# A two-block transformer kernel on one core: the opening of the first FFN by single k tiles, for four blocks, in a fixed order of vector and scalar work

## Chip, cores and metric

The kernel runs on one core of one Trainium2 chip. The metric is the device time of one execution in microseconds (us); lower is better. Before the change the median of three runs is 1663.18 us (1662.93 to 1663.85).

## What is computed

Two residual networks follow each other on one sequence x of 256 tokens and 1024 columns, in fp32. Each has two layers. What matters here is the first sublayer of the first layer: a SwiGLU FFN on a normalized and modulated x.

```python
c_act = jax.nn.silu(c)
for l in range(DEPTH):
    mod = (c_act @ w_ada[l] + b_ada[l]).reshape(B, N_SUB, 3, D_MODEL)

    def norm_mod(h, j):
        shift = mod[:, j, 0][:, None, :]
        scale = mod[:, j, 1][:, None, :]
        return _rms(h) * g_norm[l, j] * (1.0 + scale) + shift

    x = x + 0.5 * gate(0) * _swiglu(norm_mod(x, 0), w_ffn_up[l, 0], w_ffn_down[l, 0])
    x = x + gate(1) * _mixer(norm_mod(x, 1), ...)
    x = x + 0.5 * gate(2) * _swiglu(norm_mod(x, 2), w_ffn_up[l, 1], w_ffn_down[l, 1])
```

`_swiglu` is (silu(h Wg) * (h Wu)) Wd with 2816 inner columns. The second network has two layers of another mixer and another FFN, and its own modulation `w_mod_2`. Before any matmul of the first FFN can run, the kernel therefore needs x, its mean square, the row silu(c), and for each 128 columns of x the shift and the scale, which are dot products of silu(c) with rows of `w_ada`.

## The kernel before

**Precision.** TensorE multiplies fp32r, a rounded fp32. Each weight piece of 128 rows by 1024 columns (a "unit", 0.5 MB) is split into `hi` (ScalarE, a copy that rounds, L247) and `lo` = raw - hi (VectorE, L248). The activations are split in the same way into `hTh` and `hTl`, stored transposed: 8 k tiles of 128 columns of x, each 128 by 256 tokens. A product is hi*hTh + hi*hTl + lo*hTh, three matmuls.

**Weights.** `enqueue` lists loads of two units (1 MB) in the order of use, `pump` issues the load on SP's queue into one of four `raw` buffers and emits hi and lo into eight buffers each; a buffer is free again when TensorE has used its unit (`free`). 

**An FFN** works in 11 blocks of 256 inner columns. For a block, `gemm_ch` runs 4 units (2 k tiles each) with 24 matmuls of 256 columns each into two PSUM banks (gate and up), `act_ch` computes silu(gate) * up and splits it, and `down_both` runs two more units against the result. 

**Modulation.** `mod_piece` loads 1 MB of `w_ada` into a raw buffer and forms two columns of 128 dot products: on VectorE as one product with a running sum (L282), or, if `spread` says so, as a product on GpSimd (L279) and a sum on ScalarE (L280). 

**The opening** of the first FFN (`start`, `ffn_open`) handles three blocks. `start` loads silu's row c spread over 128 partitions (0.5 MB), the columns of small constants `cols`, the first w_ada piece, x and the identity, all on SP's queue, and computes the root mean square and the normalized x (`norm_in`). `ffn_open` then goes in four steps q of two k tiles: pieces for shift and scale of step q+1 (one column on VectorE, one on GpSimd and ScalarE, since `spread` is 1), hi and lo, the transposed x scaled and shifted (`norm_fill`: ScalarE L370, VectorE L375 and L376), and the matmuls of blocks 0, 1 and 2. After it, block 3 runs in the ordinary way, then the downs of blocks 0 to 2, and so on. From `hooks[3]` on, 14 pieces of w_ada for the following sublayers and some constants (`late_start`) are worked in between.

**What sets the order.** TensorE's order is the order of the program's text. The order on the other engines and queues is set by a scheduler with priorities (`high_priority`). 

```python
self.gemm_ch(ps[j], unit, q)                                     # L469
nc.gpsimd.tensor_tensor(sl, sl, self.crow, ALU.mult)             # L279
nc.scalar.activation(out=hi[:, :width], in_=r, func=ACTF.Copy)   # L247
```

Of the kernel before, what the change touches and what calls it, by code (L numbers as in the profile page):

```python
# [39 lines left out]
EXP_LN = "natural_log_exp_and_others"  # L40
GELU = "gelu_apprx_tanh_and_others"
# [32 lines left out]
LEAD = 3  # L74
MUL = 0
# [30 lines left out]
class Net:  # L106
# [54 lines left out]
    def start(self, pieces):  # L161
# [5 lines left out]
        self.ident = self.con("ident")  # L167
        self.nones = self.const.tile([P, 128], F32, name="nones")
# [7 lines left out]
        self.load_c(0)  # L176
        nc.sync.dma_start(out=self.cols, in_=self.a["cols"])
        pieces[0]()
        nc.sync.dma_start(out=self.x, in_=self.a["x"].rearrange("p (t d) -> p t d", t=2))
        nc.sync.dma_start(out=self.ident, in_=self.a["cst"][:, 0:128])  # L180
        pieces[1]()
        self.identr = self.const.tile([P, 128], F32R, name="identr")
        nc.vector.tensor_copy(self.identr, self.ident)
        with self.hot():
            return [self.norm_in(t, True) for t in range(2)]
# [7 lines left out]
    def late_start(self):  # L193
# [5 lines left out]
        nc.vector.tensor_copy(self.masks, m[:, 0:N_MASK])  # L199
        t, y, z, z2 = [self.sm(8, f"sp{i}", 1) for i in range(4)]  # L200
        lam = self.col("lam", 0, 8)
        nc.scalar.activation(out=t, in_=lam, func=ACTF.Abs)
# [16 lines left out]
        nc.vector.tensor_scalar(self.brh, self.col("b_r", 0, 16), 0.5, None, ALU.mult)  # L219
        self.gq8 = self.const.tile([P, 2], F32, name="gq8")  # L220
        nc.vector.tensor_scalar(self.gq8, self.col("g_qk", 0, 2), 0.125, None, ALU.mult)
# [9 lines left out]

    def pump(self, count=8):
# [3 lines left out]
        while self.queue and self.emitted < end:  # L236
            src, n, width = self.queue[0]
            if src is not None:
                raw = self.raw()
                nc.sync.dma_start(out=raw[:, :n * width], in_=src)  # L240
                self.cur, self.pos = raw, 0
                self.queue[0] = (None, n, width)
# [3 lines left out]
            with self.tc.high_priority(offset=0 if self.opening else -COLD):  # L246
                nc.scalar.activation(out=hi[:, :width], in_=r, func=ACTF.Copy)  # L247
                nc.vector.tensor_tensor(lo[:, :width], r, hi[:, :width].bitcast(F32), ALU.subtract)  # L248
# [6 lines left out]
    opening = True  # L255
    spread = 2
# [82 lines left out]
    def norm(self, t, ss=None, early=False):  # L339
# [5 lines left out]
        if early:  # L345
            self.nc.gpsimd.tensor_tensor(ms, ss[:, 0:1], ss[:, 1:2], ALU.add)
            self.nc.gpsimd.tensor_tensor(ms, ms, self.eps, ALU.add)
        else:
            self.nc.vector.scalar_tensor_tensor(ms, ss[:, 0:1], EPS, ss[:, 1:2], ALU.add, ALU.add)  # L349
        return self.rstd(ms, 1, "rs")  # L350

    def norm_in(self, t, scalar=False):
        r = self.norm(t, None, scalar)
        xn = []
        for n in range(2):
            h = self.s2()
            src = self.x[:, t, n * 512:(n + 1) * 512]
            if scalar and (t or MUL):
                self.nc.scalar.activation(out=h, in_=src, func=ACTF.Copy, scale=r[:, 0:1])
            else:  # L360
                self.nc.vector.tensor_scalar(h, src, r[:, 0:1], None, ALU.mult)
            xn.append(h)
# [87 lines left out]
    def ffn_open(self, xn, mod, pieces, act_ch):  # L450

        ps = [[self.up(), self.up()], [self.dn(), self.dn()], [self.dn(), self.dn()]]

        def turn(q):
            bank = self.tp()
            for t in range(2):
                for i in range(2):
                    sl = slice((q % 2 * 2 + i) * 128, (q % 2 * 2 + i + 1) * 128)
                    self.nc.tensor.transpose(bank[:, (2 * t + i) * 128:(2 * t + i + 1) * 128], xn[t][q // 2][:, sl],
# [1199 lines left out]
```

## Time and profile before

| | |
|---|---|
| median of three runs | 1663.18 us |
| the profiled execution | 1661.24 us |
| its span, first to last instruction | 1659.5 us |
| TensorE busy (PE) | 1600.4 us, 96% |
| VectorE busy (DVE) | 1273.3 us, 77% |
| ScalarE busy (ACT) | 859.7 us, 52% |
| GpSimd busy (POOL) | 69.8 us, 4% |
| granted TensorE clock, mean | 0.992 |

Engines wait for each other by semaphores. In a list of waits each row says which engine and line waited, for which instruction, for how long in all, how many times and for how long at most. In a timeline, each row has the start and the duration in us, the engine, the line of the code, the operation, the tiles written and read, the shape, a count if several instructions were merged, and in brackets how long the engine sat idle before it and which instruction ended that. Matmul durations overlap, so their pace is read from their starts.

### The profile page before, as it was taken

The numbers are of one execution on the slowest core, as the hardware profiler recorded it, in microseconds if no ns is written. First come the engines' busy times: TensorE is split into PE (matmuls) and PEld (weight loads), VectorE is DVE, ScalarE is ACT, GpSimd is POOL, SyncE is SP. The second block draws the span as 40 slices with busy tenths as digits, with TensorE's granted clock in tenths as the row PEclk, the third lists the DMA queues.
The fourth block names the chain that finished last, engine by engine and source line by source line (L and its number), as shares of the span: only waits on it lengthen the run. The fifth ranks groups of instructions, "written<-read, shape, count | busy, mean of one in ns | idle before, by whom it ended". The sixth has DMA issues, their size and how long they took to land.

```text
span 1659.5 us, 26626 instructions
## 1 busy us (share of the span) xinstructions
PE 1600.4 (96%) x10574; PEld 1448.0 (87%) x10574; DVE 1273.3 (77%) x2160; ACT 859.7 (52%) x1378; POOL 69.8 (4%) x70
## 2 busy tenths in 40 slices
PE   3899999999999999999999999999999999999998
PEld 3889987889999899989789999887899989789997
DVE  7878688679887888776689787687888776786554
ACT  4634456764344443457664445556544465564442
POOL 3100010000000000000000000001000010000000
PEclk9999999999999999999999999999999999999999
DMA  7889768449887699855349887534788854258550
GB/s 294 298 328 359 300 211 310 142 135 365 334 333 284 252 353 345 310 194 175 115 165 364 334 303 295 188 112 146 290 329 315 328 185 169 79 173 307 178 190 27
DMA packets 59325, 411.36 MB, mean 248 GB/s; under 512 B 6640, under 2 KB 7360, under 8 KB 11712
## 3 DMA queue, kind: packets, MB, share of 16 engines
q1 hardware_dynamic: 59200, 409.66, 67.0%
q8 instruction: 83, 1.36, 0.3%
q14 instruction: 42, 0.34, 0.1%
HBM read 408.54 MB, written 1.09 MB: 247 GB/s over the span
## 4 chain that ended last, share of the span: by engine, by line
PE 83%; DVE 9%; ACT 3%; issue 1%; DMA 1%; POOL 1%; SPq 0%; POOLq 0%; DVEq 0%; ACTq 0%
PE up L435 13%; PE up L436 13%; PE up L437 13%; PE dn L446 8%; PE dn L445 8%; PE dn L448 8%; DVE lo L248 3%; PE dn L421 2%; PE dn L424 2%; PE dn L422 2%; PE up L421 2%; PE up L424 2%; PE up L422 2%; DVE raw L282 1%; PE dn L437 1%
## 5 line engine op out<-in xcount | busy, mean ns | idle before, releaser
L247 ACT ACTIVATE hi<-raw 128x1024 fp32r<-128x1024 f32 (+1 forms) x508 | 527.3, 1058 | 438.3 <-PE up L436 154.2
L248 DVE TENSOR_TENSOR lo<-raw,hi 128x1024 fp32r<-128x1024 f32 (+1 forms) x508 | 618.6, 1236 | 171.0 <-ACT hi L247 167.5
L435 PE MATMUL up<-hTh,hi 128*128 128x256 f32 x1984 | 560.7, 283 | 8.4 <-DVE hTh L375 8.4
L436 PE MATMUL up<-hTl,hi 128*128 128x256 f32 x1984 | 558.0, 281 | 1.5 <-DVE hTl L376 1.5
L437 PE MATMUL up<-hTh,lo 128*128 128x256 f32 x1984 | 557.6, 281 | 0.0
L435 PEld LDWEIGHTS up<-hTh,hi 128*128 128x128 f32 x1984 | 374.3, 189 | 12.0 <-DVE hTh L375 8.8
L436 PEld LDWEIGHTS up<-hTl,hi 128*128 128x128 f32 x1984 | 374.5, 189 | 4.2 <-DVE hTl L376 2.0
L437 PEld LDWEIGHTS up<-hTh,lo 128*128 128x128 f32 x1984 | 374.6, 189 | 0.0
L282 DVE SCALAR_TENSOR_TENSOR raw<-raw,crow 128x1024 f32<-128x1024 f32 x234 | 281.3, 1228 | 3.8 <-DMA raw<-in_w_ada 3.4
L445 PE MATMUL dn<-hi,s 128*128 128x512 f32 x552 | 218.6, 396 | 0.0
L446 PE MATMUL dn<-lo,s 128*128 128x512 f32 x552 | 217.6, 394 | 0.0
L448 PE MATMUL dn<-hi,s 128*128 128x512 f32 x552 | 173.7, 394 | 0.0
L448 PEld LDWEIGHTS dn<-hi,s 128*128 128x128 f32 x552 | 103.7, 188 | 24.4
L446 PEld LDWEIGHTS dn<-lo,s 128*128 128x128 f32 x552 | 103.7, 188 | 21.5
L445 PEld LDWEIGHTS dn<-hi,s 128*128 128x128 f32 x552 | 103.7, 188 | 21.3
L533 ACT ACTIVATE s<-up 128x512 f32<-128x512 f32 (+1 forms) x60 | 32.7, 555 | 140.2 <-PE up L437 140.1
L534 DVE TENSOR_TENSOR s<-s,up 128x512 f32<-128x512 f32 (+1 forms) x60 | 37.5, 634 | 66.4 <-PE up L437 66.4
L370 ACT ACTIVATE s<-tp,shift,scale 128x128 f32<-128x128 f32 x160 | 58.6, 466 | 35.9 <-PE tp L383 26.3
L331 POOL TENSOR_TENSOR rs<-ms,mhalf 128x1 f32<-128x1 f32 x22 | 20.8, 947 | 1171.9 <-DVE ms L349 1171.7
L421 PE MATMUL dn<-hi,hTh 128*128 128x512 f32 (+2 forms) x176 | 66.2, 380 | 0.3 <-DVE hTh L375 0.3
L422 PE MATMUL dn<-lo,hTh 128*128 128x512 f32 (+2 forms) x176 | 65.2, 374 | 0.0
L424 PE MATMUL dn<-hi,hTl 128*128 128x512 f32 (+2 forms) x176 | 63.4, 375 | 0.0
(342 smaller groups left out, 1902.7 us busy)
## 6 DMA issues: line engine op xcount, KB each, us to landing
raw<-in_ffn SPq DMA_DIRECT2D x198, 1024.0 KB, 5.1
raw<-in_w_ada SPq DMA_DIRECT2D x72, 1024.0 KB, 5.2
raw<-in_mix SPq DMA_DIRECT2D x48, 1024.0 KB, 5.3
raw<-in_w_mod SPq DMA_DIRECT2D x48, 1024.0 KB, 6.8
s<-gate SPq DMA_DIRECT2D x10, 512.0 KB, 9.3
raw<-in_mix SPq DMA_DIRECT2D x4, 1032.0 KB
raw<-in_mix SPq DMA_DIRECT2D x4, 912.0 KB, 5.9
mw<-in_mix_w SPq DMA_DIRECT2D x2, 896.0 KB, 6.8
```

The lines of the kernel that those rows point to most:

```text
L247: nc.scalar.activation(out=hi[:, :width], in_=r, func=ACTF.Copy)
L248: nc.vector.tensor_tensor(lo[:, :width], r, hi[:, :width].bitcast(F32), ALU.subtract)
L282: nc.vector.scalar_tensor_tensor(sl, sl, 1.0, self.crow, ALU.mult, ALU.mult, accum_out=dst[:, b:b + 1])
L421: nc.tensor.matmul(out, xh, hi[:, sl], start=(k == 0), stop=False)
L422: nc.tensor.matmul(out, xh, lo[:, sl], start=False, stop=False)
L424: nc.tensor.matmul(out, xl, hi[:, sl], start=False, stop=(k == 7))
L435: nc.tensor.matmul(out, hi[:, sl], self.hTh[:, k], start=(k == 0 and c % 2 == 0), stop=False)
L436: nc.tensor.matmul(out, hi[:, sl], self.hTl[:, k], start=False, stop=False)
L437: nc.tensor.matmul(out, lo[:, sl], self.hTh[:, k], start=False, stop=(k == 7 and c % 2 == 1))
L445: nc.tensor.matmul(banks[t, n], xh, hi[:, sl], start=first, stop=False)
L446: nc.tensor.matmul(banks[t, n], xh, lo[:, sl], start=False, stop=False)
L448: nc.tensor.matmul(banks[t, n], xl, hi[:, n * 512:n * 512 + 512], start=False, stop=last)
```

## The change

The opening now treats four blocks (`OPEN = 4`) and one k tile at a time, eight steps instead of four.

- `start` issues loads from two engines. SP's queue gets x in two halves first, then w_ada rows and weights; ScalarE's queue gets row c as one partition (4 KB), the identity and `cols`, behind a table load for SILU.
- `open_norm` spreads row c over the partitions by two matmuls with a row of -1, takes SILU with scale -1 from PSUM, computes the mean square of x's first half on ScalarE and of the second on VectorE, and normalizes the first half on VectorE, the second on ScalarE.
- `ffn_open` loads w_ada rows for one k tile (two of 0.5 MB, in buffers of their own kind, `s4`), forms both dot products on VectorE, adds shift on ScalarE and scale on VectorE. GpSimd has no products any more. All of x is transposed at once into four banks and copied out. hTh is then written by ScalarE from the copy (in step 0 by VectorE), hTl by VectorE.
- `line` ties each vector and scalar instruction of the opening to the one before it in the program's text, so that their order there is fixed. `self.lows` holds back lo until the text asks for it.
- The weights of the first FFN are laid out for four blocks; the hooks with the 14 pieces begin at block 4. `late_start` is tied behind an activation of the FFN.

```diff
+        row = self.mw.tile([P, 1792], F32, tag="gw", name="crow0")[0:1, 0:D]
+        self.tables(SILU)
+        nc.scalar.dma_start(out=row, in_=self.a["c"][0:1, :])
+        nc.scalar.dma_start(out=self.ident, in_=self.a["cst"][:, 0:128])
+        for t in range(2):
+            nc.sync.dma_start(out=self.x[:, t], in_=self.a["x"][:, t * D:(t + 1) * D])
+        nc.scalar.dma_start(out=self.cols, in_=self.a["cols"])
...
+    def open_norm(self, row):
+
+        nc = self.nc
+        spread = [self.up(), self.up()]
+        for n in range(2):
+            nc.tensor.matmul(spread[n], self.nones[0:1, :], row[:, n * 512:(n + 1) * 512], start=True, stop=True)
+        self.crow = self.const.tile([P, D], F32, tag="crow", name="crow")
+        ss = [self.sm(1, "ss") for _ in range(2)]
+        a, v = lambda inst: self.line("a", inst), lambda inst: self.line("v", inst)
+        a(nc.scalar.activation(out=self.hTl[:, 0:4].rearrange("p k n -> p (k n)"), in_=self.x[:, 0], func=ACTF.Square,
+                               scale=1.0 / 32, accum_out=ss[0]))
+        v(nc.vector.scalar_tensor_tensor(self.hTl[:, 4:8].rearrange("p k n -> p (k n)"), self.x[:, 1], 1.0 / D,
+                                         self.x[:, 1], ALU.mult, ALU.mult, accum_out=ss[1]))
+        rs = []
+        for t in range(2):
+            ms = self.sm(1, "ms")
+            nc.gpsimd.tensor_tensor(ms, ss[t], self.eps, ALU.add)
+            rs.append(self.rstd(ms, 1, "rs"))
+        for n in range(2):
+            a(nc.scalar.activation(out=self.crow[:, n * 512:(n + 1) * 512], in_=spread[n], func=ACTF.Silu, scale=-1.0))
+        xn = [self.s4() for _ in range(2)]
+        v(nc.vector.tensor_scalar(xn[0], self.x[:, 0], rs[0][:, 0:1], None, ALU.mult))
+        for n in range(2):
+            sl = slice(n * 512, (n + 1) * 512)
+            a(nc.scalar.activation(out=xn[1][:, sl], in_=self.x[:, 1, sl], func=ACTF.Copy, scale=rs[1][:, 0:1]))
+        return xn
...
+    def line(self, engine, inst):
+
+        if self.opening:
+            self.lines = dict(self.lines)
+            if engine in self.lines:
+                self.after(inst, self.lines[engine])
+            self.lines[engine] = inst
+        return inst
...
+        def load(k):
+            landed[k] = [self.s4() for _ in range(2)]
+            for i in range(2):
+                nc.sync.dma_start(out=landed[k][i], in_=rows(i, k))
...
+        def piece(k):
+            for i, w in enumerate(landed.pop(k)):
+                if k == 0 and i == 1:
+                    v(nc.vector.tensor_scalar(plus, self.col("b_ada", 8, 8), 1.0, None, ALU.add))
+                v(nc.vector.scalar_tensor_tensor(w, w, 1.0, self.crow, ALU.mult, ALU.mult, accum_out=sums[i][:, k:k + 1]))
+            one = slice(k, k + 1)
+            a(nc.scalar.activation(out=mod["shift"][:, one], in_=sums[0][:, one], func=ACTF.Identity,
+                                   bias=self.col("b_ada", k)))
+            v(nc.vector.tensor_scalar(mod["scale"][:, one], sums[1][:, one], plus[:, one], self.col("g_norm", k), ALU.add,
+                                      ALU.mult))
+
+        load(0)
+        self.fetch(0, 2)
+        self.fetch(1)
+        load(1)
+        xn = self.open_norm(row)
...
+        def high(k, early=False):
+            g, i = k // 2, k % 2
+            src = turned[g][:, i * 256:i * 256 + 256] if early else xT[g][:, g % 2 * 512 + i * 256:g % 2 * 512 + i * 256 + 256]
+            how = dict(func=ACTF.Identity, scale=mod["scale"][:, k:k + 1], bias=mod["shift"][:, k:k + 1])
+            if early:
+                v(nc.vector.tensor_scalar(self.hTh[:, k], src, mod["scale"][:, k:k + 1], mod["shift"][:, k:k + 1], ALU.mult,
+                                          ALU.add))
+            else:
+                a(nc.scalar.activation(out=self.hTh[:, k], in_=src, **how))
+            full[k] = self.s1()
+            a(nc.scalar.activation(out=full[k], in_=src, **how))
+
+        def rest(k):
+            v(nc.vector.tensor_tensor(self.hTl[:, k], full.pop(k), self.hTh[:, k].bitcast(F32), ALU.subtract))
...
+        self.lows = []
+        piece(0)
+        self.pump(1)
+        high(0, True)
+        self.low()
...
+        for k in range(1, 8):
+            if k % 2 == 0:
+                units = self.take(OPEN)
+            if k < 7:
+                load(k + 1)
+                if k % 2:
                     self.pump(2)
-                fill(q + 1, turned[q + 1])
-            block(2, q)
-            if q < 2:
-                turned.append(turn(q + 2))
+                piece(k + 1)
+                high(k + 1)
+                if k % 2:
+                    self.low()
+                rest(k + 1)
+                if k % 2:
+                    self.low()
+                    self.pump(2)
+                    self.low(2)
+            else:
+                self.pump(4)
+                self.low(4)
+            for j in range(OPEN):
+                if k == 1 and j > 1:
+                    block(j, 0, units[j], "b")
+                block(j, k, units[j])
+                if k % 2:
+                    self.free(1)
+                if k == 7:
+                    with self.hot():
+                        act_ch(j, ps[j])
```

VectorE, the opening from the products for the second step on; `raw` or `s_` with `crow` are the products with row c, `lo` the split of weights, before first and then now:

```order
L282 SCALAR_TENSOR_TENSOR raw,shift<-raw,crow 128x1024
L376 TENSOR_TENSOR hTl<-s_168,hTh 128x2x128
L297 SCALAR_TENSOR_TENSOR shift<-shift,cols 128x2
L282 SCALAR_TENSOR_TENSOR raw,scale<-raw,crow 128x1024
L297 SCALAR_TENSOR_TENSOR scale<-scale,cols 128x2
L299 TENSOR_TENSOR scale<-scale,cols 128x2
L375 CAST hTh<-s_244 128x2x128
L376 TENSOR_TENSOR hTl<-s_244,hTh 128x2x128
L248 TENSOR_TENSOR lo<-raw,hi 128x1024 x2
```

```order
L530 SCALAR_TENSOR_TENSOR s_244,sums<-s_244,crow 128x1024
L530 SCALAR_TENSOR_TENSOR s_245,sums<-s_245,crow 128x1024
L534 TENSOR_SCALAR scale<-sums,plus,cols 128x1
L292 TENSOR_TENSOR lo<-raw,hi 128x1024
L572 TENSOR_TENSOR hTl<-s_261,hTh 128x256
L292 TENSOR_TENSOR lo<-raw,hi 128x1024 x3
L530 SCALAR_TENSOR_TENSOR s_332,sums<-s_332,crow 128x1024
L530 SCALAR_TENSOR_TENSOR s_333,sums<-s_333,crow 128x1024
L534 TENSOR_SCALAR scale<-sums,plus,cols 128x1
L572 TENSOR_TENSOR hTl<-s_341,hTh 128x256
```

Now two k tiles (steps 2 and 3) take four products, four lo, two scale steps and two hTl; in the odd step hTl follows scale with no lo between them. In the whole opening these are 16 products and 16 lo.

SP's queue, from its first load on, before first and then now:

```order
L189 DMA crow<-in_c 128x1024
L177 DMA cols<-in_cols 128x434
L274 DMA raw<-in_w_ada 128x2048
L179 DMA x<-in_x 128x2048
L180 DMA cst<-in_cst 128x128
L274 DMA raw<-in_w_ada 128x2048
L240 DMA raw<-in_ffn 128x2048
```

```order
L173 DMA x<-in_x 128x1024 x2
L518 DMA s_100<-in_w_ada 128x1024
L518 DMA s_101<-in_w_ada 128x1024
L271 DMA raw<-in_ffn 128x1024 x2
L271 DMA raw<-in_ffn 128x2048
L518 DMA s_109<-in_w_ada 128x1024
L518 DMA s_110<-in_w_ada 128x1024
L271 DMA raw<-in_ffn 128x2048 x2
L518 DMA s_244<-in_w_ada 128x1024
```

x moves from the fourth place to the first, row c and `cols` leave the queue, and the w_ada rows and the first unit go in halves of a megabyte. Up to and with `s_244`, the first row of step 2, the queue has 7.9 MB, and ScalarE's queue 0.3.

## Rows read from the trace of the kernel before

**Rows 1.** The page, busy time of TensorE, share of the span and instructions.

```profile
PE 1600.4 (96%) x10574; PEld 1448.0 (87%) x10574; DVE 1273.3 (77%) x2160; ACT 859.7 (52%) x1378; POOL 69.8 (4%) x70
```

**Rows 2.** Waits of TensorE, 0 to 100 us; total us, times, longest.

```profile
PE tp L459 <- DVE s L361: 14.4, 1, 14.4
PE up L435 <- DVE hTh L375: 8.4, 1, 8.4
...
PE tp L459 <- ACT s L359: 0.9, 1, 0.9
```

**Rows 3.** Windows, 84 to 222 us: engines busy, clock, DMA share, GB/s.

```profile
84.00:222.00 138.00, 137.77 (x924) 126.28 (x922) 104.40 (x151) 58.62 (x71) 1.07 (x1) 1.00 0.83 310
```

**Rows 4.** Timeline of TensorE, opening.

```profile
25.88 0.58 PE L435 MATMUL up<-hTh,hi 128*128 128x256 f32 x1 [8.42 <-DVE hTh L375]
...
29.44 0.41 PE L436 MATMUL up<-hTl,hi 128*128 128x256 f32 x1
29.66 0.41 PE L437 MATMUL up<-hTh,lo 128*128 128x256 f32 x1
...
34.89 0.28 PE L435 MATMUL dn<-hTh,hi 128*128 128x256 f32 x1
...
37.97 0.28 PE L437 MATMUL dn<-hTh,lo 128*128 128x256 f32 x1
...
83.51 0.39 PE L445 MATMUL dn<-hi,s 128*128 128x512 f32 x1
```

**Rows 5.** Chain of waits to 84 us: start, us, engine, what.

```profile
2.12 8.82 DMA x<-in_x
...
39.14 7.76 DMA raw<-in_w_ada
```

**Rows 6.** Timeline of VectorE, opening.

```profile
21.13 4.49 DVE L248 TENSOR_TENSOR lo<-raw,hi 128x1024 fp32r<-128x1024 f32 x2
...
28.44 0.07 DVE L282 DVE_READ_ACCUMULATOR raw<-raw,crow 128x1 f32 x1
28.62 0.16 DVE L297 SCALAR_TENSOR_TENSOR scale<-scale,cols 128x2 f32<-128x2 f32 x1
...
30.24 0.43 DVE L376 TENSOR_TENSOR hTl<-s,hTh 128x256 fp32r<-128x256 f32 x1
...
61.21 3.49 DVE L248 TENSOR_TENSOR lo<-raw,hi 128x1024 fp32r<-128x1024 f32 x3
```

**Rows 7.** Timeline of GpSimd, opening.

```profile
13.87 0.47 POOL L347 TENSOR_TENSOR ms<-ms,eps 128x1 f32<-128x1 f32 x1
14.42 0.68 POOL L331 TENSOR_TENSOR rs<-ms,mhalf 128x1 f32<-128x1 f32 x1
...
47.07 6.01 POOL L279 TENSOR_TENSOR raw<-raw,crow 128x1024 f32<-128x1024 f32 x2 [10.42 <-DMA raw<-in_w_ada]
```

**Rows 8.** Timeline of ScalarE, first instructions.

```profile
0.73 1.28 ACT L190 ACT_TABLE_LOAD   x1 [0.73 <-PEq L1648]
5.37 1.06 ACT L190 ACTIVATE crow<-crow 128x1024 f32<-128x1024 f32 x1 [3.36 <-DMA crow<-in_c]
```

**Rows 9.** Stretches before 22 us, columns as in rows 3.

```profile
2.00:4.50 2.50, 0.00 (x0) 0.00 (x0) 0.00 (x0) 0.01 (x1) 0.00 (x0) 1.00 0.70 249
4.50:22.00 17.50, 2.23 (x8) 1.43 (x8) 12.33 (x36) 10.98 (x22) 5.57 (x8) 1.00 1.01 420
```

**Rows 10.** Groups of VectorE by form: count, busy us, mean ns.

```profile
L968 DVE TENSOR_SCALAR s<-s 128x1024 f32<-128x1024 f32 x2 | 1.4, 695 | 3.0 <-ACT s L961 3.0
```

**Rows 11.** Groups of TensorE by form.

```profile
L1049 PE MATMUL dn<-s,cst 128*128 128x512 f32 x8 | 4.2, 610 | 2.6 <-DVE s L1038 2.6
```

**Rows 12.** Timeline of ScalarE, opening.

```profile
41.18 1.16 ACT L370 ACTIVATE s<-tp,shift,scale 128x128 f32<-128x128 f32 x3 [3.35 <-DVE scale L299]
```

**Rows 13.** DMA issues, 0 to 100 us: count, KB each, us to landing.

```profile
raw<-in_ffn SPq DMA_DIRECT2D x16, 1024.0 KB, 5.0
```

**Rows 14.** Stretch from 20 to 30 us, columns as in rows 3.

```profile
20.00:30.00 10.00, 3.23 (x13) 2.94 (x14) 8.92 (x13) 4.09 (x10) 4.35 (x2) 1.00 0.58 211
```

More of the change, by code (lines that the diff above doesn't have):

```diff
@@ L73 @@
 RAW = 4
-LEAD = 3
-MUL = 0
+OPEN = 4
 S4 = 8
@@ L159, in con, with start @@
         return self.cst[:, o:o + w]
-    def start(self, pieces):
+    def start(self):
         nc = self.nc
@@ L175, in start @@
         self.hTl = self.const.tile([P, 8, S], F32R, name="hTl")
[L176 to L185, printed above, removed]
+        return row
+    def open_norm(self, row):
[23 more added lines that the diff above has]
+        return xn
     def load_c(self, i):
@@ L230, in enqueue, with fetch @@
             self.queue.append((src[:, i * width:(i + n) * width], n, width))
+    fetched = None
+    def fetch(self, at, parts=1):
+        src, n, width = self.queue[at]
+        if self.fetched is None:
+            self.fetched = {}
+        if id(src) in self.fetched:
+            return self.fetched.pop(id(src))[1]
+        raw = self.raw()
+        for i in range(parts):
+            sl = slice(i * n * width // parts, (i + 1) * n * width // parts)
+            self.nc.sync.dma_start(out=raw[:, sl], in_=src[:, sl])
+        if parts > 1 or at:
+            self.fetched[id(src)] = src, raw
+        return raw
     def pump(self, count=8):
@@ L255, with low @@
     opening = True
+    lines = ()
+    def line(self, engine, inst):
+        if self.opening:
+            self.lines = dict(self.lines)
[3 more added lines that the diff above has]
+        return inst
+    def low(self, n=1):
+        for _ in range(n):
+            self.lows.pop(0)()
     spread = 2
@@ L344, in norm, with norm_in @@
         ms = self.sm(1, "ms")
[L345 to L349, printed above, removed]
+        self.nc.vector.scalar_tensor_tensor(ms, ss[:, 0:1], EPS, ss[:, 1:2], ALU.add, ALU.add)
         return self.rstd(ms, 1, "rs")
-    def norm_in(self, t, scalar=False):
-        r = self.norm(t, None, scalar)
+    def norm_in(self, t):
+        r = self.norm(t)
         xn = []
@@ L490, in ffn_open @@
         self.opening = False
-        self.spread = 2
         self.pump(4)
-        for j in range(3):
-            with self.hot():
-                act_ch(j, ps[j])
     def ffn(self, mod, hooks, nxt, opening=None):
@@ L589, in ffn @@
             nd = 1
-        start = 2 if opening is None else 3
+        start = 2 if opening is None else OPEN
         for h in sum(hooks[:start], []):
@@ L1405, in body, with first_rows @@
         self.pending = {}
-        xn = self.start([shifts[0][0], shifts[0][4]])
+        row = self.start()
+        def first_rows(i, k):
+            return a["w_ada"][0][2 * i + k // 4][:, k % 4 * 1024:k % 4 * 1024 + 1024]
         flat = list(gates[0])
```

123 lines of the change are left out of this document (73 added, 50 removed).

## The prediction

> **What bounds the kernel now.** I read the waits of TensorE first, because TensorE is busy 96% of the span [rows 1]. In the first 100 us it waits 29.5 us in six groups: 14.4 us for the normalized x, 8.4 us for hTh, three more for hi, hTl and lo, and 0.9 us for x again [rows 2]. From 84 to 222 us, the rest of the first FFN, it is busy 137.77 of 138.00 us while VectorE is busy 104.40 and the loads take 0.83 of the DMA engines [rows 3]. So what can be won in this FFN is won before 84 us, and nothing behind it waits for anything but TensorE.
>
> The timeline of TensorE gives the size of the opening. The first matmul of the FFN starts at 25.88, the first down matmul at 83.51 [rows 4]. Between them lie four blocks of 96 matmuls of 256 columns. At full clock 26 of them take 37.97 - 34.89 = 3.08 us, 0.1185 each, so 384 take 45.5 us. The missing 57.6 - 45.5 = 12.1 us are the later waits and stretches at half clock (1.2 of 2.4 GHz), for instance from 29.44 to 29.66, 0.21 us a matmul [rows 4].
>
> The chain of waits up to 84 us says what fed them late [rows 5]: x lands after 8.8 us in the queue, and further down a w_ada load of 7.8 us comes too late. The timeline of VectorE shows a second cost: a pair of lo that starts at 21.1, beside GpSimd's products with row c, takes 4.49 us, and three that start at 61.2 take 3.49, which is 1.15 from start to start [rows 6]. GpSimd has six such products, the last two from 47.1 to 53.1 [rows 7].
>
> **The change, step by step.** The opening now treats one k tile of 128 at a time, for four blocks, and every step follows from VectorE's list. So I add up that list and put TensorE behind it.
>
> *Start.* The first half of x is the first load of SP's queue. The nearest row is row c before: also half a megabyte, also first, used at 5.37 [rows 8]. So x's first half is there at 5.4, the second 0.52 MB at 420 GB/s [rows 9] later, at 6.6. VectorE squares it with its sum (1.22 us and 0.08, as lo and a read of the sum in [rows 6]): 7.9. GpSimd then adds eps (0.47) and takes the first root (0.68) [rows 7]: 9.1. One TENSOR_SCALAR of 1024 columns is 0.70 [rows 10]: the products with row c begin at 9.8.
>
> *Row c.* It comes by ScalarE's queue, is spread by two fp32 matmuls of 512 columns (0.6 us each at full clock [rows 11], twice that at half) and passes two SILU of some 0.6. ScalarE first loads a table (1.28 us from 0.73 [rows 8]). I bound its landing from two sides: some 5 us, if it doesn't stand behind SP's loads; or 10, behind 2.6 MB of them. The nearest row is the 64 KB identity, which stood behind x in one queue; here the queue is its own, so I take 5. Then the spread row is ready at some 8, under the cover of x's sums until 9.8. Landing at 10 it would be ready at 13, and 3 us would show, less the wait for loads that I add below. The Trainium skill (DMA: Bandwidth & Descriptors, Issuing engines are not separate DMA queues) says that loads started by different engines interleave on the same DMA engines and that a second engine saves issue time only. By that the bandwidth stays at 420 GB/s and the early landing of the small row holds; no row of before shows a second queue.
>
> *VectorE from 9.8 to the last hTl.* From the order of the change: 16 products with c at 1.15 from start to start, 18.4; 16 lo at 1.15, 18.4, now that GpSimd has no products; hTh once and hTl eight times at some 0.4, 3.7; eight scale steps, each 0.12 until the sum is there and 0.17, 2.4 [rows 6]. Further three waits for ScalarE: in steps 3, 5 and 7 no lo stands between scale and hTl, so VectorE waits for two ACTIVATEs of 256 columns, 0.1 + 0.36 + 0.46 + 0.06 = 1.0 each (0.35 apart in pairs of 128 columns before [rows 12]), 3.0. And one wait for loads: up to the first row of step 2 the queues move 8.2 MB, of which 0.5 are there at 5.4; 7.6 MB at 420 GB/s are 18.2, landing at 23.6, while VectorE is ready after 4 products, 4 lo and the small steps, 11.0 us, at 20.8: 2.8. Sum 18.4 + 18.4 + 3.7 + 2.4 + 3.0 + 2.8 = 48.7: the last hTl is ready at 58.5.
>
> *Loads behind that.* Until the last step they are 18.1 MB, 43 us at 420 GB/s. The order gives two steps of rows and two raw buffers ahead, so I cost later waits at nothing.
>
> *TensorE.* Its first FFN matmul starts at some 13, after two products, scale and hTh. A pair of steps is 96 matmuls, 11.4 us, against 11.6 of VectorE's list (eight at 1.15, two hTl, two scale steps, one wait), so it keeps up and ends 5.6 us (46 matmuls that come after the last hTl, and 0.1 to start) behind it: 64.1, against 83.51. **Gain 19.4 us.** The SILU table is there from the start, so the 1.28 us load that came with the first SILU of the FFN goes; it lay beside TensorE's work, nothing.
>
> *What follows.* Block 4 needs four units. Two lo precede the first SILU product on VectorE, the third and fourth follow by 65; TensorE takes 2.8 us a unit, so it doesn't wait. The 14 w_ada pieces now lie in four blocks. VectorE's 104 us in 138 [rows 3] stay; its share is the same, for all of the FFN moves forward. The late constants with two table loads (2.6 us of ScalarE, half idle) hide too. Behind the first FFN every engine's order is unchanged. So the 19.4 us reach the end: the profiled execution of 1661.24 us (span 1659.5) would take 1641.8. The median of the runs, 1663.18, lies 1.9 above it: **1643.8 us**.
>
> **Rivals.** *Half-size loads are slow.* x, the w_ada rows and the first unit now move in half megabytes. Between 2 and 4.5 us, when mostly row c (half a megabyte) moved, the rate was 249 GB/s, against 420 later [rows 9]. If all 10.5 MB of such loads move at 249 and the other 7.6 MB at 420, the last rows land at 2 + 42.2 + 18.1 = 62. Behind them come a product, scale, hTh and hTl (3.0) and the last step (5.7): 71, a gain of 12.5, 1650.7. Against it: row c was read 128 times from one place, and the queue had only just started. The Trainium skill (same page, Bandwidth) states the rule "Batch DMAs to ≥1 MiB for ≥75% of peak", which speaks against this change; by its fit of 2.0 us plus the bytes at 436 GB/s, an estimate, half a megabyte takes 3.2 us, the twenty such loads 64 us if one followed the other, and the opening would end at some 91, slower than now. The 1 MB loads of before take 5 us to land and still sum to 420 GB/s [rows 9, 13], so they overlap; I give the rival 0.13.
>
> *TensorE stays at half clock.* Before, it ran at half clock for a while after its first FFN matmul [rows 4]. Here the first two steps have waits for hi and lo between their matmuls. If their 96 matmuls all run at 0.213, they end at 13.4 + 20.4 = 33.8 and TensorE sets the pace from there: 288 x 0.1185 = 34.1, 67.9, 3.8 us later than forecast, 1647.6. Otherwise TensorE catches up before step 3, since VectorE is the slower. 0.08.
>
> *Loads wait for buffers, and it gets slower.* Row and raw buffers come free only as VectorE works through its list, and SP issues in order: a load that waits for its buffer holds up all behind it. Before, the loads moved at 211 GB/s from 20 to 30 us [rows 14]. The 18.1 MB at 211 are 86 us; the last rows land at 88 and the opening ends at 97, 13 us later than now: 1676.6. The point from which it decides: below 250 GB/s over the whole opening, the last rows land after 75 and nothing is gained. Against it: six row buffers and four raw buffers run ahead, and that stretch of before lies beside GpSimd's products, when VectorE was slow. 0.04.
>
> *The gain doesn't reach the end.* If VectorE fell behind in blocks 4 to 10, TensorE would wait there, where it had no wait. That takes 16 us of new waits in a stretch where VectorE has 34 us to spare: 1660 to 1666. 0.03.
>
> **How the numbers follow.** Forecast 0.72: an opening that ends between 59 and 68. At the low end the waits for loads and ScalarE (5.8 us) vanish; then TensorE's own 45.5 us from 13 set the end, 59, so 1639. The high end takes in half-size loads at 249 GB/s, so the range is 1639 to 1651; the half clock and a late row c lie within. Outside are the two last rivals and some of the first, less than 2 in 10. About 0.2% (3.3 us) is what a measurement can tell from no change: faster 0.93 (forecast and the first two rivals), the same 0.03, slower 0.04.
>
> **What would show it.** Right: the first FFN matmul at about 13; lo at 1.22 us everywhere; TensorE's waits in the first 100 us some 15 to 17 us, most of them before 13; the first product of step 2 waiting for a w_ada load by some 2 to 3 us; three waits of hTl for ScalarE of 1 us; block 4 from about 64; no wait of TensorE from there to the end of the first FFN, some 202 us. Wrong: products waiting for w_ada loads in step after step (first or third rival), 0.21 us a matmul after 27 us (second), or a wait of TensorE for lo or hi after 64 (last).

## The result and the profile after

The changed kernel takes 1642.05 us (median of 4 runs, 1641.78 to 1644.12), against 1663.06 us (1660.17 to 1663.85) for the kernel before beside it: a ratio of 0.9879, 95% interval 0.9862 to 0.9897. The forecast was 1643.8 us. The change itself was timed a second time later, beside other runs: 1642.82 against 1660.69 us. In the profiled execution, of 1641.78 us (span 1640.0), TensorE is busy 1601.5 us, one more than before [rows 1]: what went was idle time.

The waits of TensorE from 0 to 100 us, 29.5 us before [rows 2], are 9.3 us:

```profile
PE tp L547 <- DVE s L206: 2.7, 1, 2.7
PE up L190 <- DMA crow<-in_c: 2.6, 1, 2.6
PE up L584 <- ACT hTh L567: 1.4, 2, 1.0
PE up L584 <- ACT hi L289: 1.3, 1, 1.3
PE up L584 <- DVE hTl L572: 1.3, 3, 0.4
```

Its timeline, to set against [rows 4]: the first FFN matmul starts at 13.99 instead of 25.88, and block 4, which follows the opening, at 67.38 instead of 83.51. At 37.65 comes the last wait of the opening; soon after it, matmuls are 0.21 us apart for a while.

```profile
13.99 1.22 PE L584 MATMUL up<-hTh,hi 128*128 128x256 f32 x4 [1.29 <-ACT hi L289]
...
36.69 0.39 PE L584 MATMUL up<-hTh,hi 128*128 128x256 f32 x1 [1.03 <-ACT hTh L567]
...
37.65 0.39 PE L584 MATMUL up<-hTl,hi 128*128 128x256 f32 x1 [0.45 <-DVE hTl L572]
...
39.07 0.41 PE L584 MATMUL up<-hTh,lo 128*128 128x256 f32 x1
39.28 0.41 PE L584 MATMUL up<-hTl,hi 128*128 128x256 f32 x1
...
67.38 0.28 PE L491 MATMUL up<-hTh,hi 128*128 128x256 f32 x1
```

The timeline of VectorE, to set against [rows 6], has its list. It waits for w_ada loads three times, and in the odd steps for ScalarE before hTl. Three lo take 3.49 us as before, but no group is drawn out to 4.49 for a pair.

```profile
11.37 1.23 DVE L530 SCALAR_TENSOR_TENSOR s<-s,crow 128x1024 f32<-128x1024 f32 x1 [1.17 <-DMA s<-in_w_ada]
...
17.91 1.23 DVE L530 SCALAR_TENSOR_TENSOR s<-s,crow 128x1024 f32<-128x1024 f32 x1 [1.24 <-DMA s<-in_w_ada]
...
25.45 1.23 DVE L530 SCALAR_TENSOR_TENSOR s<-s,crow 128x1024 f32<-128x1024 f32 x1 [1.95 <-DMA s<-in_w_ada]
...
29.85 3.49 DVE L292 TENSOR_TENSOR lo<-raw,hi 128x1024 fp32r<-128x1024 f32 x3
...
37.16 0.43 DVE L572 TENSOR_TENSOR hTl<-s,hTh 128x256 fp32r<-128x256 f32 x1 [1.22 <-ACT s L569]
...
60.97 0.42 DVE L572 TENSOR_TENSOR hTl<-s,hTh 128x256 fp32r<-128x256 f32 x1 [1.22 <-ACT s L569]
```

The stretches, with the columns of [rows 3]. From 20 to 30 us the loads move 411 GB/s (211 before [rows 14]), and from block 4 to 202 us TensorE is busy all the time, as before [rows 3].

```profile
4.50:22.00 17.50, 12.70 (x61) 10.03 (x59) 11.89 (x20) 11.46 (x20) 1.71 (x4) 1.00 1.02 390
20.00:30.00 10.00, 8.95 (x69) 7.99 (x67) 7.74 (x14) 4.90 (x8) 0.00 (x0) 1.00 1.02 411
67.38:202.00 134.62, 134.62 (x915) 124.06 (x914) 109.31 (x174) 61.60 (x74) 0.00 (x0) 1.00 0.88 328
```

### The profile page after: what moved, and what is told of

It reads as the page before. It is cut to its first block, busy times and chain, and to the rows that moved or that the text cites. A ratio compares the mean times of both kernels' runs of the same rounds, so it can differ in the third digit from the quotient of the medians.

```text
span 1640.0 us, 26615 instructions
## 1 busy us (share of the span) xinstructions
PE 1601.5 (98%) x10578; PEld 1446.6 (88%) x10578; DVE 1267.4 (77%) x2163; ACT 856.3 (52%) x1372; POOL 52.5 (3%) x62
## 4 chain that ended last, share of the span: by engine, by line
PE 84%; DVE 9%; ACT 3%; DMA 2%; issue 1%; POOL 1%; SPq 0%; POOLq 0%; ACTq 0%; DVEq 0%
PE up L491 13%; PE up L492 13%; PE up L493 13%; PE dn L501 8%; PE dn L502 8%; PE dn L504 8%; DVE lo L292 2%; PE dn L477 2%; PE dn L480 2%; PE dn L478 2%; PE up L477 2%; PE up L480 2%; PE up L478 2%; PE dn L584 1%; DMA s<-in_w_ada 1%
## 5 line engine op out<-in xcount | busy, mean ns | idle before, releaser
L292 DVE TENSOR_TENSOR lo<-raw,hi 128x1024 fp32r<-128x1024 f32 (+1 forms) x508 | 609.7, 1221 | 160.9 <-ACT hi L289 157.2
L491 PE MATMUL up<-hTh,hi 128*128 128x256 f32 x1920 | 540.8, 282 | 0.0
L492 PE MATMUL up<-hTl,hi 128*128 128x256 f32 x1920 | 538.0, 280 | 0.0
L493 PE MATMUL up<-hTh,lo 128*128 128x256 f32 x1920 | 537.9, 280 | 0.0
L491 PEld LDWEIGHTS up<-hTh,hi 128*128 128x128 f32 x1920 | 361.1, 188 | 3.2 <-issue 0.2
L492 PEld LDWEIGHTS up<-hTl,hi 128*128 128x128 f32 x1920 | 361.6, 188 | 2.1
L493 PEld LDWEIGHTS up<-hTh,lo 128*128 128x128 f32 x1920 | 361.5, 188 | 0.0
L345 DVE SCALAR_TENSOR_TENSOR raw<-raw,crow 128x1024 f32<-128x1024 f32 x224 | 267.5, 1221 | 2.6 <-DMA raw<-in_w_ada 2.3
L426 ACT ACTIVATE s<-tp,shift,scale 128x128 f32<-128x128 f32 x144 | 52.0, 466 | 26.4 <-PE tp L439 26.4
## 6 DMA issues: line engine op xcount, KB each, us to landing
s<-in_w_ada SPq DMA_DIRECT2D x16, 512.0 KB, 12.6
```

Source lines behind the costliest of these rows:

```text
L292: self.line("v", nc.vector.tensor_tensor(lo[:, :width], r, hi[:, :width].bitcast(F32), ALU.subtract))
L345: nc.vector.scalar_tensor_tensor(sl, sl, 1.0, self.crow, ALU.mult, ALU.mult, accum_out=dst[:, b:b + 1])
L491: nc.tensor.matmul(out, hi[:, sl], self.hTh[:, k], start=(k == 0 and c % 2 == 0), stop=False)
L492: nc.tensor.matmul(out, hi[:, sl], self.hTl[:, k], start=False, stop=False)
L493: nc.tensor.matmul(out, lo[:, sl], self.hTh[:, k], start=False, stop=(k == 7 and c % 2 == 1))
```

## The experiments

All but the last two runs are read from their traces, by one mark: the start of the first matmul behind the opening, called the end of the opening here (83.51 us before, 67.38 in the change). The two executions of the change differ by 0.3 us in this mark, those of the kernel before by 1.7, so a difference of some tenths between single executions says little. The total times of these runs are single executions too, and differ by some us for reasons told further down.

**The kernel before again.** 

> The kernel before, unchanged, once more. Theory: the change acts in the first 84 us alone, and what differs between two executions behind that is drift. Then this execution's marks (first gate transposes 184.9 us, last ones 1612.5 us) may differ from the first execution's by 1 to 2 us at the end and by at most 0.3 at the first mark. Rival: the 1.9 us by which the gain grows behind 320 us are the change's own; then the marks of this execution lie within 0.3 us of the first one's everywhere.

The opening ended at 81.86 us, the first gate transposes came at 183.28 (184.93 in the first execution) and the last at 1611.83 (1612.49). So the rival's 0.3 us fails at once: two executions of one kernel differ by 1.7 us in the opening. But the theory fails too, for the difference is largest at the first mark (1.7 us, not 0.3) and shrinks to 0.7 at the last, not 1 to 2. How far the gain grows behind it is taken up under "point by point".

**x first in the old opening**, the only part of the change that this run has.

```diff
-        self.load_c(0)
-        nc.sync.dma_start(out=self.cols, in_=self.a["cols"])
-        pieces[0]()
         nc.sync.dma_start(out=self.x, in_=self.a["x"].rearrange("p (t d) -> p t d", t=2))
         nc.sync.dma_start(out=self.ident, in_=self.a["cst"][:, 0:128])
+        self.load_c(0)
+        nc.sync.dma_start(out=self.cols, in_=self.a["cols"])
+        pieces[0]()
```

> The kernel before with one part of the change alone: x and the identity are the first loads, ahead of row c and the first two megabytes of w_ada. Theory: the first FFN matmul of the old opening needs x, row c and two 1 MB loads of w_ada together, and the order of these bytes doesn't change their sum, so the transposes come early (some 10 us instead of 16) but the first FFN matmul stays at 24 to 26 us and the opening ends at 81 to 83.5. Rival: the wait for x was what set the opening, and x first brings a large part of the gain by itself: opening ends below 77.

The transposes began at 9.05 us, but the first FFN matmul at 25.70 and the opening ended at 81.75, as in the run above. The 14.4 us of [rows 2] turned into other waits of the same length:

```profile
PE up L435 <- DVE hTh L375: 9.7, 1, 9.7
PE tp L459 <- DVE s L361: 9.0, 1, 9.0
PE tp L459 <- ACT s L359: 4.7, 1, 4.7
```

The largest wait of a list may be worth nothing, when the one behind it comes at a fixed time.

**GpSimd helps again.**

```diff
+                if k and i:
+                    nc.gpsimd.tensor_tensor(w, w, self.crow, ALU.mult)
+                    continue
                 v(nc.vector.scalar_tensor_tensor(w, w, 1.0, self.crow, ALU.mult, ALU.mult, ...
...
+            if k:
+                a(nc.scalar.activation(out=w, in_=w, func=ACTF.Identity, accum_out=sums[1][:, one]))
```

> The change with one part undone: in steps 1 to 7 GpSimd multiplies the scale rows and ScalarE sums them, VectorE keeps the shift rows. Theory: VectorE's list gets shorter by 7 products of 1.15 us but its work beside GpSimd slows (a pair of lo took 4.49 us there before, instead of 2.4), and a scale step comes after 3.0 us of GpSimd and 1.0 of ScalarE, some 2 us later than now in steps 1 to 3. The opening ends at 69 to 72 us (67.5 now). Rival: the list of VectorE sets the pace to the end, and any help shortens it: below 65.5.

The opening ended at 76.34 us, 9.0 later, and the time was 1651.27. The direction is the theory's, the size at least twice its own. VectorE's rows show why: it waits 3.5 us for the sum, and beside GpSimd's product (29.02 to 31.41, then 33.05 to 36.24) one lo takes 2.25 us and three take 5.70.

```profile
30.06 0.27 DVE L539 TENSOR_SCALAR scale<-sums,plus,cols 128x1 f32<-128x1 f32 x1 [3.46 <-ACT s L538]
30.25 2.25 DVE L292 TENSOR_TENSOR lo<-raw,hi 128x1024 fp32r<-128x1024 f32 x1
...
32.76 5.70 DVE L292 TENSOR_TENSOR lo<-raw,hi 128x1024 fp32r<-128x1024 f32 x3
```

A pair of steps takes 14.7 us from hTl to hTl (42.43 to 57.12), against 11.9 in the change. I had added the theory's terms for the first steps only; the pair pays them every time. The last hTl ended at 70.77 us, 9.4 later than in the change, and the opening 5.6 behind it, so the loss is in VectorE's list.

**No fixed order.**

```diff
-            if engine in self.lines:
-                self.after(inst, self.lines[engine])
```

> The change without the fixed order: line() no longer ties an instruction of VectorE or ScalarE to the one before, so the scheduler orders them. VectorE then normalizes x behind two products and two lo, and the hTl of steps 1 to 3 each come behind the products of a later step. Theory: the first FFN matmul starts at some 21 us instead of 14.0, the hTl of step 2 comes some 4.5 us later, and the opening ends at 69 to 72 us. Rival: the loads bind until 26 us and VectorE's list has the same sum in any order, so the opening ends at 67 to 68 as now.

The first FFN matmul started at 20.34 us, the hTl of step 2 came at 33.90 (29.51 in the change), and the opening ended at 68.90. The first two numbers are the theory's; the third lies 0.1 below its range and 1.5 above the change. But its mechanism is another one here: the last hTl ended at 60.65 us, before that of the change (61.39), and the opening 8.3 behind it. TensorE waited for nothing from 22.18 us to the end of the opening, so with its late start its own work set the end. The time of 1648.49 us is not due to that: 4.2 of the 6.7 us by which its span is longer lie behind the second gate transposes (309 us), where no instruction is in another place.

**x behind the first rows.**

```diff
-        for t in range(2):
-            nc.sync.dma_start(out=self.x[:, t], in_=self.a["x"][:, t * D:(t + 1) * D])
...
         load(0)
+        for t in range(2):
+            nc.sync.dma_start(out=self.x[:, t], in_=self.a["x"][:, t * D:(t + 1) * D])
         self.fetch(0, 2)
```

> The change with x loaded behind the first pair of w_ada rows instead of ahead of it. Theory: until 26 us the opening waits for the rows of step 2 (used at 25.45), behind which VectorE works without a gap to the hTl of step 3 (37.2) and TensorE from there to the end. A megabyte of x later moves the first FFN matmul from 14.0 to some 18, but VectorE then no longer waits 1.2 us at 17.9 and 2.0 at 25.5, so the rows of step 2 are used at some 26.5 and the opening ends at 68 to 69 us (67.4 now). Rival: the first FFN matmul sets the end, and 4 us later there are 4 us later at the end: 71 to 72.

Both missed. The first FFN matmul was 2.3 us later (16.24), and yet the opening ended 1.7 us earlier, at 65.66. So the first matmul doesn't set the end, as long as it doesn't come as late as in the run above. The rows of step 2 were there when VectorE came to them, at 24.30 instead of 25.45, and everything behind them came earlier by that much or more:

```profile
24.30 1.22 DVE L528 SCALAR_TENSOR_TENSOR s<-s,crow 128x1024 f32<-128x1024 f32 x1
...
59.66 0.42 DVE L572 TENSOR_TENSOR hTl<-s,hTh 128x256 fp32r<-128x256 f32 x1 [1.22 <-ACT s L569]
```

The rate of the loads is not the reason. They moved 395 GB/s from 7 to 10 us in this run and 262 to 304 in the change, but here the dip lies from 4 to 7 us instead (218 to 332), and by 10 us both had moved 2.6 MB. Why the rows of step 2, issued 2.5 us later than in the change (13.91 against 11.43), are there at least 1.15 us earlier is open, and so are the dips.

**Row c by a broadcast load.**

```diff
-        row = self.mw.tile([P, 1792], F32, tag="gw", name="crow0")[0:1, 0:D]
+        row = self.mw.tile([P, 1792], F32, tag="gw", name="crow0")[:, 0:D]
...
-        nc.scalar.dma_start(out=row, in_=self.a["c"][0:1, :])
+        nc.scalar.dma_start(out=row, in_=self.a["c"][0:1, :].to_broadcast([P, D]))
```

The two matmuls that spread the row go too. 

> The change with row c read to 128 partitions by its load (0.5 MB, still by ScalarE's queue) instead of a 4 KB row spread by two matmuls. Theory: the loads are the bound until 26 us, so half a megabyte more (1.2 us at 420 GB/s) makes the rows of step 2 come 1.2 us later and the opening ends at 68.3 to 69. Rival: the queue of ScalarE takes a share that SP's loads leave free (262 to 304 GB/s moved from 7 to 10 us), and the opening ends at 67.1 to 67.7 as now.

The x halves came 1.9 and 2.3 us later (used at 6.72 and 8.51), the rows of step 2 0.84 later (26.29), the last hTl at 61.81 instead of 60.97, and the opening ended at 67.79, between the two ranges. The 4 KB row is worth 0.8 us on VectorE's list. At the end it is 0.4 us against the change, which was held up by a stretch at half clock from 38.23, and 0.7 against its second execution (67.11), which like this run has no such stretch.

**A lo in every gap.**

```diff
                 high(k + 1)
-                if k % 2:
-                    self.low()
+                self.low()
                 rest(k + 1)
                 if k % 2:
                     self.low()
                     self.pump(2)
-                    self.low(2)
+                    self.low()
```

> The change with one lo put between scale and hTl in steps 3, 5 and 7 too, so that VectorE no longer waits there for ScalarE (3 times 1.2 us). Theory: TensorE is the bound from the hTl of step 3 on, so only the first of the three waits can count, and the fourth lo of step 2 now comes behind the products of step 3, where TensorE may wait for it: the opening ends at 66.5 to 68 us (67.4 now). Rival, the sum of the prediction: VectorE's list sets the pace to the last hTl, and 3.6 us less of it end the opening at 63.5 to 64.5.

The last hTl started at 58.06 us, 2.9 earlier, but the opening ended only 1.1 earlier, at 66.25. The theory missed by 0.25 us, the rival by 1.75. TensorE pays for the fourth lo where the theory had it, and the opening ends 7.8 us behind the end of the last hTl, not 5.6 to 6.0 as in the change:

```profile
36.50 0.38 PE L584 MATMUL tp<-hTh,lo 128*128 128x256 f32 x1 [1.63 <-DVE lo L292]
```

**Three blocks.** OPEN = 3, with one lo less per pair of steps. 

> The change with three blocks in the opening (OPEN = 3, as many as before); block 3 follows whole. Theory: with three blocks a pair of steps is 8.5 us of TensorE but 10.8 of VectorE, which sets the pace from 25.5 us on; the last hTl comes at some 58, the three blocks end at 62 and block 3 at 73 to 74.5 (67.4 now), 6 us later. Rival: the early first matmul by single k tiles is the whole gain, and three blocks do as well as four: block 3 ends before 69.

The three blocks ended at 61.65 us and block 3 at 72.96, 5.6 later than block 3 of the change; these are about the theory's numbers. VectorE's list without the fourth lo is shorter by only 1.15 us in 11.9, and TensorE has a quarter less to do beside it.

**The rows of step 2 early.** They were issued from 11.4 us on, behind 2 MB of weights, because all eight buffers of their size were taken. Now they go to the place of a constant that is loaded late, and to the tile of row c.

```diff
-            landed[k] = [self.s4() for _ in range(2)]
+            landed[k] = [self.s4() for _ in range(2)] if k != 2 else [self.cst[:, 128:128 + D], self.gw0]
```

> The change with the rows of step 2 loaded into two buffers that are free from the start, so that SP issues them ahead of the 2 MB of weights of steps 2 and 3. Theory, as corrected by the run with x behind the rows: it is the landing of these rows (25.45 us) that sets the hTl of steps 2 and 3, not the sum of all loads. They land by 22, VectorE doesn't wait for them, the hTl of step 3 comes at some 35.5 instead of 37.2, and the opening ends at 64 to 66 us (67.4 now). Rival: the loads are the bound by their bytes; the weights that now come behind the rows make hi and lo of step 2 late instead, and the opening ends at 67 to 68.

The wait at 25.45 is gone (the product starts at 23.06), and the opening ended at 64.65, 2.7 us earlier; the rival's late hi and lo don't show among TensorE's waits, which from 15 us on are for hTl.

```profile
23.06 1.22 DVE L531 SCALAR_TENSOR_TENSOR cst<-cst,crow 128x1024 f32<-128x1024 f32 x1
```

**Four edits together.** 

> The run before, and three edits more: the rows of step 1 too are issued ahead of the second megabyte of weights, only 192 of the 434 columns of cols are loaded at the start, and in steps 3, 5 and 7 VectorE makes hTh itself while ScalarE makes the full product. Theory: the first FFN matmul stays at 14.0 or comes up to 0.5 earlier, VectorE waits for loads by under 2.5 us in all (4.4 now), and TensorE is its own bound from 22 us on: 384 matmuls at 0.1185 are 45.5 us, with some 2.5 us of slow start and 1.5 of waits the opening ends at 62.5 to 64.5. Rival: TensorE's waits in steps 1 and 2 stay what they are, since hTh of step 1 stands behind four hi on ScalarE: 65 to 67.

The opening ended at 64.25 us, within the theory's range, and VectorE waited only 0.4 us for loads. But it gained nothing by the rows of step 1: hi of blocks 2 and 3 became late, as TensorE's waits show, and ScalarE's work of step 1 stands behind them. VectorE waits 2.3 us for hi (1.0 in the run before), and 2.0 us in step 1 for ScalarE's full product, where it had no wait. The smaller cols did not lift the rate from 7 to 10 us either (280 GB/s).

```profile
PE dn L586 <- ACT hi L291: 1.1, 1, 1.1
PE tp L586 <- ACT hi L291: 0.7, 1, 0.7
PE up L586 <- ACT hi L291: 0.6, 1, 0.6
```

**The change again, and the best version**, timed side by side. The best version is the run before with the rows of step 1 back behind the second megabyte of weights. Its further edits:

```diff
-        nc.scalar.dma_start(out=self.cols, in_=self.a["cols"])
+        nc.scalar.dma_start(out=self.cols[:, 0:192], in_=self.a["cols"][:, 0:192])
...
-                high(k + 1)
+                high(k + 1, k % 2 == 0)
```

and the rows of step 2 as above. 

> The change itself once more, timed beside the next run. Theory: the opening ends at 67.4 us within 1.7 (one stretch at half clock more or less), and the ratio to the kernel before stays at 0.987 to 0.989. Rival: part of the 19.5 us was one lucky execution, and the ratio comes out above 0.990.

> The combined run without the edit that cost it something there (the rows of step 1 stay behind the weights of step 0): rows of step 2 in buffers of their own, 192 columns of cols, hTh of steps 3, 5 and 7 by VectorE. Theory: the hi of blocks 2 and 3 come in time again (the waits of 1.1 and 0.7 us for them go), TensorE waits for hTl of step 3 no more, and the opening ends at 63.0 to 64.5 us; the time lies 2 to 4 us below that of the change. Rival: without that edit the rows of step 1 are 1.2 us late again, the two cancel, and the opening ends at 64.2 to 65.5.

The change took 1642.82 us (ratio 0.9894, 0.9879 to 0.9909, just above the theory's 0.987 to 0.989 and below the rival's 0.990; opening 67.11), the best version 1639.05 us (ratio 0.9873, 0.9856 to 0.9889; opening 62.87, just below the theory's range). The second is 3.8 us faster by the medians of 4 runs each, whose ranges don't overlap (1641.51 to 1644.42, and 1638.42 to 1640.47).

The change again also settles who sets the pace. Its trace has no stretch at half clock in the opening after 18 us, and TensorE waits for hTl in steps 5 and 7 as well:

```profile
49.69 0.39 PE L584 MATMUL up<-hTl,hi 128*128 128x256 f32 x1 [0.33 <-DVE hTl L572]
...
61.59 0.39 PE L584 MATMUL up<-hTl,hi 128*128 128x256 f32 x1 [0.33 <-DVE hTl L572]
...
67.11 0.28 PE L491 MATMUL up<-hTh,hi 128*128 128x256 f32 x1
```

So the theory's words "TensorE is the bound from the hTl of step 3 on" were too strong: in the change the two engines run neck and neck, 11.9 us a pair for VectorE and 11.4 for TensorE, and VectorE's list sets the end wherever TensorE isn't held up by itself. In the change, its second run, the run with GpSimd, that with x behind the rows, that with row c broadcast, that with the rows of step 2 early, the combined run and the best version, the opening ends 5.6 to 6.0 us behind the end of the last hTl. The two runs in which TensorE sets the end are that with a lo in every gap (7.8) and that without fixed order (8.3).

## Why the prediction was right, point by point

The time came out 1.8 us below the forecast, within the range, and the mechanism was the predicted one: the matmuls start 12 us earlier, and VectorE's list with TensorE 5.6 to 6.0 us behind it sets the end of the opening. The opening itself gained less than the 19.4 us forecast: 83.51 to 67.38 is 16.1, and between the second executions of both kernels (81.86 to 67.11) it is 14.8. That the whole time still fits so closely is luck, as told below.

- **Start.** Right to within 1 us: x's halves were used at 4.79 and 6.18 (5.4 and 6.6 forecast), products began at 8.89 (9.8), the first FFN matmul at 13.99 (some 13). That the matmul is later although the products are earlier comes from two waits for loads that had no term: VectorE's second product waited 1.17 us for its row, so hTh was ready only at 13.60, and hi, whose raw load came at 12.88, at 13.94.
- **Row c costs nothing.** Right. Its spread matmuls began at 2.59, earlier than either of my bounds, and row c itself was ready at 7.0, before the first product at 8.89. The price of the spread was read too low: the two matmuls are four records of TensorE and took 3.75 us, not 1.2 to 2.4, which the early landing paid for. The Trainium skill's rule (DMA: Bandwidth & Descriptors, Issuing engines are not separate DMA queues) agrees with the bandwidth: 390 GB/s from 4.5 to 22 us, below and not above the 420 of before [rows 9].
- **VectorE's list.** From the first product to the last hTl it took 52.5 us (8.89 to 61.39), where the sum had 48.7. Waits for loads were 4.4 in three places, not 2.8 in one; waits for ScalarE 3.7, not 3.0; 0.4 for hi had no term; the remaining work was 44.1, not 42.9. The largest miss is the loads: the waits of 1.17 and 1.24 us for the rows of steps 0 and 1 had no term, and the first row of step 2 was used at 25.45, not 23.6. Its bytes were counted right, for 8.3 MB had moved by 23.6 us; but a count of bytes doesn't give the landing of one load among those in the queue. Issued ahead of the 2 MB of weights, in the run with these rows early, the row was there by 23.06, when VectorE came to it. The last hTl ended at 61.4, not 58.5.
- **TensorE behind it.** 5.6 us forecast, 6.0 measured, 5.6 in the second run. That it keeps up is right only just: 37.65 is its last wait of the opening in the profiled execution, where a stretch at half clock then held it up by some 1.5 us; without it, in the second execution, it waits for hTl in steps 5 and 7 too.
- **Where the waits are.** Forecast 15 to 17 us in the first 100, measured 9.3: I hadn't counted that TensorE starts on the spread matmuls and the transposes early.
- **What follows.** No wait of TensorE from block 4 until 206.57 us, as forecast. But the gain was not simply carried to the end. In the profiled executions it is 16.7 us at the first gate transposes (184.93 to 168.27) and 19.4 at the last (1612.49 to 1593.13). Behind the first FFN every engine's order is the same in both kernels. Some 1.1 of these 2.7 us are systematic: over three traces of the old opening and eleven of the new one, four of the nine stretches between gate transposes are shorter in every trace of the new one than in any of the old, by 0.17 to 0.43 us by their medians, 1.1 together. For instance, between the eighth and the ninth, with all engines' work equal and no wait of TensorE,

```profile
1302.05:1407.97 105.92, 105.92 (x722) 97.38 (x721) 75.47 (x135) 59.00 (x114) 5.92 (x7) 1.00 0.63 225
```

before, and after

```profile
1283.26:1388.72 105.46, 105.46 (x722) 96.94 (x721) 75.44 (x135) 58.97 (x114) 5.92 (x7) 1.00 0.62 226
```

  (105.90 to 105.92 in all three of the old, 105.39 to 105.71 in the new). Matmul by matmul, the 0.46 us build up in some ten steps of 0.04 us, spread over the stretch and at no wait. Why is open; no run was made for it. The rest is within the difference from one execution to the next. So the forecast of 19.4 us met the measured 19.5 (1659.5 - 1640.0) with an opening worth 3.3 us less and a remainder worth 3.4 more, for which the prediction had no term: two errors that cancel. By the medians of the two sets of runs the whole gain is 21.0 and 17.9 us.
- **The rivals.** Half-size loads are not slow: 390 GB/s from 4.5 to 22 us and 411 from 20 to 30, when they were half and three quarters of the bytes. The Trainium skill's "Batch DMAs to ≥1 MiB for ≥75% of peak" (same page, Bandwidth) does not decide here, where the loads overlap; a half-size w_ada load takes 12.6 us from issue to landing (median of those issued in the first 30 us). Loads didn't get slower for want of buffers, but the want of buffers set their order, the milder form of the third rival. Matmuls 0.21 us apart end at 17.75 us here. With the stretch from 38.23 the slow clock costs TensorE some 2.5 us, and some 1 in the second execution, an estimate at 0.1 us a slow matmul from 15.59 on; VectorE's list hides most of it, for the two openings end 0.3 us apart. GpSimd's products, which the prediction blamed for VectorE's slow lo, are confirmed as a cost by the run that brings them back.

## What to carry to other kernels

Add up the list of the engine that feeds the bottleneck and put the waits into it: the opening's end follows the last item of that list by a fixed time, as long as the bottleneck still waits for the items. Where it doesn't (a lo too late for it, a first matmul at 20.3 us), its own sum sets the end. Neither the largest wait (x first alone: 0) nor an earlier first matmul (2.3 us later, 1.7 us faster) tells what an edit is worth. For loads, count not only the bytes but look where a load stands in the queue and which buffer lets it be issued: two free buffers for the next step's rows were worth 2.7 us. Compare such edits by a mark in the trace right behind the place, since the whole time has several us of other causes in it.

## What the runs showed of the hardware

**Half clock comes at other places in each execution.** The granted clock falls to half (1.2 of 2.4 GHz) for 3.4 or 6.8 us at a time; one of 3.4 us costs a busy TensorE 1.5 to 1.7 us. In the openings such a stretch begins at 38.2 us in the change, nowhere after 18 us in its second execution, at 59.7 in one execution of the old kernel and at 45.1 in the other. Row of the change:

```profile
38.00:41.40 3.40, 3.40 (x19) 3.40 (x18) 3.28 (x6) 2.33 (x6) 0.00 (x0) 0.53 1.01 381
```

The engine had waited 1.03 and 0.45 us just before, but the same two waits in the repeated run brought no such stretch. Behind the opening they come five to seven times a run. The run without fixed order has one of 6.8 and one of 3.4 us between 790 and 812 us, where the change has one of 3.4, and another at 1101. The two stretches between gate transposes in which these lie are 4.7 us longer than in the change, which covers the 4.2 us by which it falls behind after 309 us:

```profile
1100.00:1106.00 6.00, 5.92 (x25) 3.83 (x23) 5.22 (x26) 1.57 (x6) 0.00 (x0) 0.72 0.01 4
```

**A clock of 1.00 in a row can mean that there is no record of it.** After TensorE's first FFN matmuls the kernel before has matmuls 0.21 us apart until 32.4 us, or until 31.4 in its second execution, in rows that say 1.00:

```profile
27.00:32.00 5.00, 4.65 (x21) 4.65 (x22) 3.35 (x9) 2.93 (x5) 1.09 (x1) 1.00 0.87 347
```

But the first clock record of these traces begins only at 32.35 and 31.47 us, just where the pace goes to 0.12 us, and a stretch without a record counts as 1.00. In the change and its second execution the pace goes to 0.12 at the first record too (17.75 and 18.00). In five runs the first record begins before the first FFN matmul (12.4 to 14.6 us), and there the pace is 0.12 at once. A pace of 0.21 is also that of the stretch recorded at half clock from 38.23. So the early stretch was most likely at half clock, as the prediction read it; no record says so.

**A short load on a second queue lands ahead of a long one on the first.** Row c was issued by ScalarE at 0.76 us, beside its table load, and was used at 2.59, while x's first half, issued by SP at 0.74, was used at 4.79. No run has row c on SP's queue, so whether its size or its queue does this is not shown; the 64 KB identity, next on ScalarE's queue, took 5.0 us to land.

```profile
2.59 3.75 PE L190 MATMUL up<-crow,nones 1*128 1x512 f32 x4 [2.59 <-DMA crow<-in_c]
```
